# A weighted sum over experts: 128 consecutive tokens per partition, one weights transfer, longer store runs and a reshaped tail

## The chip, the cores and the metric

The kernel runs on one core of a Trainium2 chip. The metric is the time of one execution on the device in microseconds (us), as the median of several runs. Beside it there is a profile of one execution, whose span is a little shorter than the measured time because it starts with the first recorded instruction. The core has a vector engine (VectorE, DVE in the profile), a scalar engine (ScalarE, ACT), GpSimd (POOL), SyncE (SP, here used to issue transfers only), and 16 DMA engines that move data between the memory outside the core (HBM) and the on-chip memory (SBUF), which has 128 partitions.

## The reference

Every token has eight expert outputs of 512 numbers and eight weights. The result is the weighted sum over the experts, all in float32.

```python
batch, seq, n_experts, expert_dim = 16, 1024, 8, 512
expert_outputs   # (16, 1024, 8, 512) float32, 268.4 MB
combine_weights  # (16, 1024, 8)      float32, 0.5 MB

def reference(expert_outputs, combine_weights):
    weights = combine_weights[..., np.newaxis]
    return np.sum(expert_outputs * weights, axis=2).astype(np.float32)   # 33.6 MB
```

There are 16 x 1024 = 16384 tokens. A token's input is 8 x 512 x 4 bytes = 16 KiB, its output 2 KiB. Each input number is used once, with one multiplication and one addition.

## The kernel before

A step handles 256 tokens: 128 partitions with two consecutive tokens (J = 2) each. Partition p of step n holds tokens 256 n + 2 p and 256 n + 2 p + 1, so one load of 4 MiB reads one contiguous piece of HBM, as 128 runs of 32 KiB, each 32 KiB behind the one before. A store writes 512 KiB as 128 runs of 4 KiB. The layout is in the three views:

```python
P = 128
J = 2
n_steps = T // (P * J)          # 64
eo_blk = expert_outputs.rearrange("b s e d -> (b s) e d").rearrange("(n p j) e d -> n p j e d", p=P, j=J)
w_blk  = combine_weights.rearrange("b s e -> (b s) e").rearrange("(n p j) e -> n p j e", p=P, j=J)
o_blk  = out.rearrange("b s d -> (b s) d").rearrange("(n p j) d -> n p j d", p=P, j=J)
in_pool  = ...   # bufs=4, 32 KiB per partition each
out_pool = ...   # bufs=4, 4 KiB per partition each
load_engines = [nc.sync, nc.scalar]
```

Loads alternate between the queues of SyncE and ScalarE and run three steps ahead. The weights of a step come in a small transfer of their own from GpSimd. The last two steps are loaded token by token:

```python
def issue_load(m):
    in_t = in_pool.tile([P, J, E, D], fp32, name="in_t")
    w_t = w_pool.tile([P, J, E], fp32, name="w_t")
    if m < n_steps - K_TAIL:                                   # K_TAIL = 2
        load_engines[m % 2].dma_start(out=in_t, in_=eo_blk[m])                 # line 56
    else:
        for j in range(J):
            load_engines[m % 2].dma_start(out=in_t[:, j], in_=eo_blk[m, :, j]) # line 59
    nc.gpsimd.dma_start(out=w_t, in_=w_blk[m])                                 # line 60
```

In 62 of the 64 steps VectorE does all the work: for each token one product and seven fused multiply-adds over 512 numbers. The store goes out on the queue that the step's load did not use.

```python
for n in range(n_steps):
    if n + LA < n_steps:                 # LA = 3
        issue_load(n + LA)
    ...                                  # the last two steps are left to the tail below
    acc = out_pool.tile([P, J, D], fp32)
    for j in range(J):
        nc.vector.tensor_scalar_mul(out=acc[:, j, :], in0=in_tile[:, j, 0, :], scalar1=w_tile[:, j, 0:1])  # line 77
        for e in range(1, E):
            nc.vector.scalar_tensor_tensor(                                                                # line 83
                out=acc[:, j, :], in0=in_tile[:, j, e, :], scalar=w_tile[:, j, e:e+1], in1=acc[:, j, :],
                op0=mult, op1=add)
    load_engines[(n + 1) % 2].dma_start(out=o_blk[n], in_=acc)                                             # line 92
```

In the last two steps ScalarE makes the products of four of the eight experts in bf16 (line 111), VectorE does the other four (lines 116 and 122), adds the bf16 products up (lines 130, 135 and 138), and each token is stored by itself on SyncE's queue (line 141).

Of the kernel before, what the change touches and what calls it, by code (L numbers as in the profile page):

```python
# [1 line left out]

# [4 lines left out]


@with_exitstack  # L10
def kernel(
    ctx: ExitStack,
    tc: tile.TileContext,
    expert_outputs: bass.AP,
    combine_weights: bass.AP,
    out: bass.AP,
):
    nc = tc.nc
    fp32 = mybir.dt.float32
    bf16 = mybir.dt.bfloat16  # L20

    B, S, E, D = expert_outputs.shape
    T = B * S
    P = 128
    J = 2
    n_steps = T // (P * J)

    eo_blk = expert_outputs.rearrange("b s e d -> (b s) e d").rearrange(
        "(n p j) e d -> n p j e d", p=P, j=J
    )  # L30
    w_blk = combine_weights.rearrange("b s e -> (b s) e").rearrange(
        "(n p j) e -> n p j e", p=P, j=J
    )
    o_blk = out.rearrange("b s d -> (b s) d").rearrange(
        "(n p j) d -> n p j d", p=P, j=J
    )

    in_pool = ctx.enter_context(tc.tile_pool(name="in_pool", bufs=4))
    w_pool = ctx.enter_context(tc.tile_pool(name="w_pool", bufs=4))
    out_pool = ctx.enter_context(tc.tile_pool(name="out_pool", bufs=4))  # L40
    prod_pool = ctx.enter_context(tc.tile_pool(name="prod_pool", bufs=2))

    ES = E // 2
    K_TAIL = 2

    load_engines = [nc.sync, nc.scalar]

    LA = 3
    in_tiles: list[bass.AP | None] = [None] * n_steps
    w_tiles: list[bass.AP | None] = [None] * n_steps  # L50

    def issue_load(m: int) -> None:
        in_t = in_pool.tile([P, J, E, D], fp32, name="in_t")
        w_t = w_pool.tile([P, J, E], fp32, name="w_t")
        if m < n_steps - K_TAIL:
            load_engines[m % 2].dma_start(out=in_t, in_=eo_blk[m])
        else:
            for j in range(J):
                load_engines[m % 2].dma_start(out=in_t[:, j], in_=eo_blk[m, :, j])
        nc.gpsimd.dma_start(out=w_t, in_=w_blk[m])  # L60
        in_tiles[m] = in_t
        w_tiles[m] = w_t

    for m in range(min(LA, n_steps)):
        issue_load(m)

    for n in range(n_steps):
        if n + LA < n_steps:
            issue_load(n + LA)
        if n >= n_steps - K_TAIL:  # L70
            continue
        in_tile = in_tiles[n]
        w_tile = w_tiles[n]
        acc = out_pool.tile([P, J, D], fp32)

        for j in range(J):
            nc.vector.tensor_scalar_mul(  # L77
                out=acc[:, j, :],
                in0=in_tile[:, j, 0, :],
                scalar1=w_tile[:, j, 0:1],  # L80
            )
            for e in range(1, E):
                nc.vector.scalar_tensor_tensor(  # L83
                    out=acc[:, j, :],
                    in0=in_tile[:, j, e, :],
                    scalar=w_tile[:, j, e : e + 1],
                    in1=acc[:, j, :],
                    op0=mybir.AluOpType.mult,
                    op1=mybir.AluOpType.add,
                )  # L90

        load_engines[(n + 1) % 2].dma_start(out=o_blk[n], in_=acc)  # L92

    tail_steps = list(range(n_steps - K_TAIL, n_steps))
    tail_accs = {}
    tail_prods = {}
    for n in tail_steps:
        acc = out_pool.tile([P, J, D], fp32, name="acc")
        prods = prod_pool.tile([P, J, E - ES, D], bf16, name="prods")
        tail_accs[n] = acc  # L100
        tail_prods[n] = prods

    for j in range(J):
        for n in tail_steps:
            in_tile = in_tiles[n]
            w_tile = w_tiles[n]
            acc = tail_accs[n]
            prods = tail_prods[n]

            for e in range(ES, E):  # L110
                nc.scalar.mul(  # L111
                    out=prods[:, j, e - ES, :],
                    in_=in_tile[:, j, e, :],
                    mul=w_tile[:, j, e : e + 1],
                )
            nc.vector.tensor_scalar_mul(  # L116
                out=acc[:, j, :],
                in0=in_tile[:, j, 0, :],
                scalar1=w_tile[:, j, 0:1],
            )  # L120
            for e in range(1, ES):
                nc.vector.scalar_tensor_tensor(  # L122
                    out=acc[:, j, :],
                    in0=in_tile[:, j, e, :],
                    scalar=w_tile[:, j, e : e + 1],
                    in1=acc[:, j, :],
                    op0=mybir.AluOpType.mult,
                    op1=mybir.AluOpType.add,
                )
            nc.vector.tensor_add(  # L130
                out=prods[:, j, 0:2, :],
                in0=prods[:, j, 0:2, :],
                in1=prods[:, j, 2:4, :],
            )
            nc.vector.tensor_add(  # L135
                out=prods[:, j, 0, :], in0=prods[:, j, 0, :], in1=prods[:, j, 1, :]
            )
            nc.vector.tensor_add(  # L138
                out=acc[:, j, :], in0=acc[:, j, :], in1=prods[:, j, 0, :]
            )  # L140
            nc.sync.dma_start(out=o_blk[n, :, j], in_=acc[:, j, :])


# [1 line left out]
_INS = ['expert_outputs', 'combine_weights']  # L145
_OUTS = [((16, 1024, 512), 'float32')]


# [23 lines left out]
```

## Time and profile before

The median of three runs is 721.33 us (721.21 to 722.09). The profile has this to say:

| What | Number |
|---|---|
| Span of the profiled execution | 720.4 us |
| VectorE busy | 644.4 us (89%), 1020 instructions |
| ScalarE busy | 11.4 us (2%) |
| GpSimd busy (issuing weights) | 35.8 us (5%) |
| HBM read / written | 268.96 MB / 33.55 MB |
| Mean DMA rate over the span | 420 GB/s |
| Loads of 4096 KB | 62, about 33 us from issue to landing |
| Stores of 512 KB | 62, about 33 us from issue to landing |
| Stores of 256 KB (tail) | 4, 3.0 us |

The profile is read in this way. "Busy" is the time in which an engine worked on an instruction. The slices cut the span into 40 equal parts and give the busy share of each in tenths; the line of GB/s is what the DMA engines moved. The chain of waits follows the work that ended last back to the start and says which engine or transfer each part of the span waited for. A group is all instructions of one line with the same operation: after the bar stand busy time in us, mean ns of one, and the idle time of the engine just before them with what ended it. A transfer's "issue to landing" includes the time in which it stood behind others in its queue.

### The profile page before, as it was taken

The page shows a single profiled execution, that of the slowest core. Times are in us where ns is not written, and L with a number is a line of the kernel's source. Part 1 is how long each engine was busy: PE and PEld are TensorE (multiplying, and loading weights), DVE is VectorE, ACT ScalarE, POOL GpSimd, SP SyncE. Part 2 cuts the span into 40 slices and gives each one's busy share as a digit, 9 for nine tenths or more (in the row PEclk, how much of TensorE's full clock was granted, in tenths as well). Part 3 has the DMA queues.
Part 4 walks back from the last instruction along what each step waited for, and adds up shares of the span by engine and source line. Part 5 has one row for each costly group of instructions (what it writes and reads, how often), then busy time and mean ns, then how long its engine had stood idle before and what let it go on. Part 6 is the DMA issues. An engine that isn't in the chain of part 4 may idle for free.

```text
span 720.4 us, 1532 instructions
## 1 busy us (share of the span) xinstructions
DVE 644.4 (89%) x1020; ACT 11.4 (2%) x17; POOL 35.8 (5%) x68
## 2 busy tenths in 40 slices
DVE  0799999999998999989998999989998999999977
ACT  0000000000000000000000000000000000000023
POOL 1000000000000000000000000000000000000000
DMA  9999999999999999999999999999999999999993
GB/s 380 437 416 451 427 426 430 427 424 439 443 431 426 426 423 431 438 436 434 431 423 426 435 430 442 432 424 427 430 429 432 442 431 428 430 425 428 433 359 120
DMA packets 21068, 302.63 MB, mean 420 GB/s; under 512 B 3136, under 2 KB 4160, under 8 KB 12608
## 3 DMA queue, kind: packets, MB, share of 16 engines
q1 hardware_dynamic: 9792, 151.52, 49.2%
q10 hardware_dynamic: 9216, 150.47, 48.9%
q0 software_dynamic: 2048, 0.53, 0.3%
q14 instruction: 12, 0.10, 0.0%
HBM read 268.96 MB, written 33.55 MB: 420 GB/s over the span
## 4 chain that ended last, share of the span: by engine, by line
DMA 63%; DVE 35%; issue 1%; DVEq 0%; SPq 0%
DMA out_dram<-acc 56%; DVE acc L83 30%; DMA in_t<-in_expert_outputs_dram 8%; DVE acc L77 3%; DVE acc L122 1%; DVE acc L138 0%; DVE prods L130 0%; DVE acc L116 0%; DVE prods L135 0%; DVEq L77 0%; DVEq L116 0%; SPq L92 0%
## 5 line engine op out<-in xcount | busy, mean ns | idle before, releaser
L83 DVE SCALAR_TENSOR_TENSOR acc<-in_t,w_t,acc 128x512 f32<-128x512 f32 x868 | 580.1, 743 | 0.0
L77 DVE TENSOR_SCALAR acc<-in_t,w_t 128x512 f32<-128x512 f32 x124 | 54.6, 482 | 66.3 <-DMA in_t<-in_expert_outputs_dram 43.4
L60 POOL DMA_DIRECT2D w_t<-in_combine_weights_dram x64 | 35.6, 556 | 637.7 <-DVE acc L83 636.9
L111 ACT ACT_TABLE_LOAD x1 | 1.3, 1283 | 690.6 <-DMA in_t<-in_expert_outputs_dram 690.6
L111 ACT ACTIVATE prods<-in_t,w_t 128x512 bf16<-128x512 f32 x16 | 10.1, 709 | 9.0 <-DMA in_t<-in_expert_outputs_dram 9.0
L122 DVE SCALAR_TENSOR_TENSOR acc<-in_t,w_t,acc 128x512 f32<-128x512 f32 x12 | 8.9, 745 | 0.0
L116 DVE TENSOR_SCALAR acc<-in_t,w_t 128x512 f32<-128x512 f32 x4 | 1.9, 481 | 5.3 <-DMA out_dram<-acc 5.3
L138 DVE TENSOR_TENSOR acc<-acc,prods 128x512 f32<-128x512 f32 x4 | 2.8, 688 | 0.0
L130 DVE TENSOR_TENSOR prods<-prods 128x1024 bf16<-128x1024 bf16 x4 | 2.7, 683 | 0.0
L135 DVE TENSOR_TENSOR prods<-prods 128x512 bf16<-128x512 bf16 x4 | 1.7, 417 | 0.0
L156 POOL MEMSET const-float32-0.0<- 128x1 f32 x1 | 0.1, 99 | 0.2 <-issue 0.2
L156 POOL MEMSET const-bfloat16-1.0<- 128x1 bf16 x1 | 0.1, 102 | 0.0
L156 POOL MEMSET const-float32-1.0<- 128x1 f32 x1 | 0.1, 99 | 0.0
L156 POOL MEMSET const-uint8-127<- 128x1 uint8 x1 | 0.1, 99 | 0.0
## 6 DMA issues: line engine op xcount, KB each, us to landing
in_t<-in_expert_outputs_dram ACTq DMA_DIRECT2D x31, 4096.0 KB, 33.5
in_t<-in_expert_outputs_dram SPq DMA_DIRECT2D x31, 4096.0 KB, 33.3
out_dram<-acc ACTq DMA_DIRECT2D x31, 512.0 KB, 33.5
out_dram<-acc SPq DMA_DIRECT2D x31, 512.0 KB, 33.4
in_t<-in_expert_outputs_dram SPq DMA_DIRECT2D x2, 2048.0 KB, 31.2
in_t<-in_expert_outputs_dram ACTq DMA_DIRECT2D x2, 2048.0 KB, 13.9
w_t<-in_combine_weights_dram POOLq DMA_DIRECT2D x64, 8.0 KB, 6.9
out_dram<-acc SPq DMA_DIRECT2D x4, 256.0 KB, 3.0
```

Source lines behind the costliest of these rows:

```text
L60: nc.gpsimd.dma_start(out=w_t, in_=w_blk[m])
L77: nc.vector.tensor_scalar_mul(out=acc[:, j, :], in0=in_tile[:, j, 0, :], scalar1=w_tile[:, j, 0:1],)
L83: nc.vector.scalar_tensor_tensor(out=acc[:, j, :], in0=in_tile[:, j, e, :], scalar=w_tile[:, j, e : e + 1], in1=acc[:, j, :], op0=mybir.Al ...
L111: nc.scalar.mul(out=prods[:, j, e - ES, :], in_=in_tile[:, j, e, :], mul=w_tile[:, j, e : e + 1],)
L116: nc.vector.tensor_scalar_mul(out=acc[:, j, :], in0=in_tile[:, j, 0, :], scalar1=w_tile[:, j, 0:1],)
L122: nc.vector.scalar_tensor_tensor(out=acc[:, j, :], in0=in_tile[:, j, e, :], scalar=w_tile[:, j, e : e + 1], in1=acc[:, j, :], op0=mybir.Al ...
L130: nc.vector.tensor_add(out=prods[:, j, 0:2, :], in0=prods[:, j, 0:2, :], in1=prods[:, j, 2:4, :],)
L135: nc.vector.tensor_add(out=prods[:, j, 0, :], in0=prods[:, j, 0, :], in1=prods[:, j, 1, :])
L138: nc.vector.tensor_add(out=acc[:, j, :], in0=acc[:, j, :], in1=prods[:, j, 0, :])
L156: nc = _bacc.Bacc("TRN2", target_bir_lowering=False, num_devices=1)
```

## The change

The layout changes: a partition owns 128 consecutive tokens (K = 128), and there are 128 partitions, so that all 16384 tokens make one block (N = 1). A load still brings two tokens for every partition, as 128 runs of 32 KiB, but these runs are now 128 x 16 KiB = 2 MiB apart in HBM. In this layout eight tokens of a partition (G = 8) are neighbours in the output, so a store can write them as one run of 16 KiB, and all weights of a partition are one run of 4 KiB, so they come in one transfer. The first product of each token moves from VectorE to ScalarE. All loads go out on SyncE's queue, most stores on ScalarE's. The last loads shrink, in the end to one expert of one token, and so do the last stores, so that little is left to do after the last bytes have come. The bf16 products of the tail are gone.

```diff
-    J = 2
-    n_steps = T // (P * J)
+    K = 128
+    G = 8
+    J = 2
+    N = T // (P * K)
...
-        "(n p j) e d -> n p j e d", p=P, j=J
+        "(n p k) e d -> n p k e d", p=P, k=K
...
-    in_pool = ctx.enter_context(tc.tile_pool(name="in_pool", bufs=4))
-    w_pool = ctx.enter_context(tc.tile_pool(name="w_pool", bufs=4))
-    out_pool = ctx.enter_context(tc.tile_pool(name="out_pool", bufs=4))
-    prod_pool = ctx.enter_context(tc.tile_pool(name="prod_pool", bufs=2))
+    in_pool = ctx.enter_context(tc.tile_pool(name="in_pool", bufs=5))
+    w_pool = ctx.enter_context(tc.tile_pool(name="w_pool", bufs=1))
+    out_pool = ctx.enter_context(tc.tile_pool(name="out_pool", bufs=2))
...
+    w_t = w_pool.tile([P, N, K, E], fp32, name="w_t")
+    chunks = [(n, k) for n in range(N) for k in range(0, K, J)]
+    last = len(chunks) - 1
+    pin = tc.keep_in_program_order
+
+    def load(i):
+        n, k = chunks[i]
+        t = in_pool.tile([P, J, E, D], fp32, name="in_t")
+        src = x[n, :, k : k + J]
+        if i < last - 6:
+            nc.sync.dma_start(out=t, in_=src)
+            return
+        for j in range(J):
+            if i == last and j == J - 1:
+                cuts = (0, 2, 4, 5, 6, 7, 8)
+            elif i >= last - 2:
+                cuts = (0, 4, 8)
+            else:
+                cuts = (0, 8)
+            for a, b in zip(cuts, cuts[1:]):
+                nc.sync.dma_start(out=t[:, j, a:b], in_=src[:, j, a:b])
...
+    def first(i):                      # acc is a tile [P, G, D]; a is the place of the chunk in it
+        for j in range(J):
+            pin(nc.scalar.mul(out=acc[:, a + j], in_=in_tiles[i][:, j, 0], mul=w_t[:, n, k + j, 0:1]))
+
+    def rest(i):
+        for j in range(J):
+            for e in range(1, E):
+                nc.vector.scalar_tensor_tensor(
+                    out=acc[:, a + j], in0=in_tiles[i][:, j, e],
+                    scalar=w_t[:, n, k + j, e : e + 1], in1=acc[:, a + j], op0=mult, op1=add)
+
+    def store(i):                      # put(queue, lo, hi) stores tokens lo to hi of acc
+        if i < last - 3:
+            if a == G - J:
+                put(nc.scalar, 0, G)
+        elif a == 2:
+            put(nc.scalar, 0, 4)
+        elif a == 4:
+            put(nc.sync, 4, 6)
+        elif a == 6:
+            put(nc.sync, 6, 7)
+            put(nc.sync, 7, 8)
...
+    AHEAD = 4
+    load(0)
+    nc.scalar.dma_start(out=w_t.rearrange("p n k e -> p n (k e)"), in_=w)
+    for i in range(1, AHEAD):
+        load(i)
+    first(0)
+    for i in range(len(chunks)):
+        if i + AHEAD <= last:
+            load(i + AHEAD)
+        if i < last:
+            first(i + 1)
+        rest(i)
+        store(i)
```

Some lines of the diff are joined or left out here; the sizes, queues and order are as they stand in it.

More of the change, by code (lines that the diff above doesn't have):

```diff
@@ L19 @@
     fp32 = mybir.dt.float32
-    bf16 = mybir.dt.bfloat16
+    mult, add = mybir.AluOpType.mult, mybir.AluOpType.add
     B, S, E, D = expert_outputs.shape
@@ L24 @@
     P = 128
+    K = 128
+    G = 8
     J = 2
-    n_steps = T // (P * J)
-    eo_blk = expert_outputs.rearrange("b s e d -> (b s) e d").rearrange(
-        "(n p j) e d -> n p j e d", p=P, j=J
-    )
-    w_blk = combine_weights.rearrange("b s e -> (b s) e").rearrange(
-        "(n p j) e -> n p j e", p=P, j=J
-    )
-    o_blk = out.rearrange("b s d -> (b s) d").rearrange(
-        "(n p j) d -> n p j d", p=P, j=J
-    )
-    in_pool = ctx.enter_context(tc.tile_pool(name="in_pool", bufs=4))
@@ L39 @@
-    w_pool = ctx.enter_context(tc.tile_pool(name="w_pool", bufs=4))
-    out_pool = ctx.enter_context(tc.tile_pool(name="out_pool", bufs=4))
-    prod_pool = ctx.enter_context(tc.tile_pool(name="prod_pool", bufs=2))
[L43 to L74, printed above, removed]
-        for j in range(J):
[L77 to L80, printed above, removed]
-            )
+    N = T // (P * K)
@@ new lines @@
+    x = expert_outputs.rearrange("b s e d -> (b s) e d").rearrange(
+        "(n p k) e d -> n p k e d", p=P, k=K
+    )
+    w = combine_weights.rearrange("b s e -> (b s) e").rearrange(
+        "(n p k) e -> p n (k e)", p=P, k=K
+    )
+    o = out.rearrange("b s d -> (b s) d").rearrange("(n p k) d -> n p k d", p=P, k=K)
+    in_pool = ctx.enter_context(tc.tile_pool(name="in_pool", bufs=5))
+    w_pool = ctx.enter_context(tc.tile_pool(name="w_pool", bufs=1))
+    out_pool = ctx.enter_context(tc.tile_pool(name="out_pool", bufs=2))
@@ new lines @@
+    w_t = w_pool.tile([P, N, K, E], fp32, name="w_t")
+    chunks = [(n, k) for n in range(N) for k in range(0, K, J)]
+    last = len(chunks) - 1
+    in_tiles = {}
+    accs = {}
+    pin = tc.keep_in_program_order
+    def load(i):
+        n, k = chunks[i]
+        t = in_pool.tile([P, J, E, D], fp32, name="in_t")
+        in_tiles[i] = t
+        src = x[n, :, k : k + J]
+        if i < last - 6:
+            nc.sync.dma_start(out=t, in_=src)
+            return
+        for j in range(J):
+            if i == last and j == J - 1:
[6 more added lines that the diff above has]
+                nc.sync.dma_start(out=t[:, j, a:b], in_=src[:, j, a:b])
@@ new lines, in acc_of @@
+    def acc_of(i):
+        n, k = chunks[i]
+        g = (n, k // G)
+        if g not in accs:
+            accs[g] = out_pool.tile([P, G, D], fp32, name="acc")
+        return accs[g], k % G
+    def first(i):
+        n, k = chunks[i]
+        acc, a = acc_of(i)
+        for j in range(J):
+            pin(
+                nc.scalar.mul(
+                    out=acc[:, a + j],
+                    in_=in_tiles[i][:, j, 0],
+                    mul=w_t[:, n, k + j, 0:1],
+                )
+            )
@@ L82 @@
+    def rest(i):
+        n, k = chunks[i]
+        acc, a = acc_of(i)
+        for j in range(J):
             for e in range(1, E):
                 nc.vector.scalar_tensor_tensor(
[L84 to L89, printed above, removed]
-                )
-        load_engines[(n + 1) % 2].dma_start(out=o_blk[n], in_=acc)
@@ L94 @@
[L94 to L141, printed above, removed]
@@ new lines, in rest, with put @@
+                    out=acc[:, a + j],
+                    in0=in_tiles[i][:, j, e],
+                    scalar=w_t[:, n, k + j, e : e + 1],
+                    in1=acc[:, a + j],
+                    op0=mult,
+                    op1=add,
+                )
+    def store(i):
+        n, k = chunks[i]
+        acc, a = acc_of(i)
+        k0 = k - a
+        def put(queue, lo, hi):
+            pin(queue.dma_start(out=o[n, :, k0 + lo : k0 + hi], in_=acc[:, lo:hi]))
+        if i < last - 3:
[8 more added lines that the diff above has]
+            put(nc.sync, 7, 8)
```

## The prediction

> **What bounds the kernel now.** I read the page's slices first, then the queue totals, then the chain of waits, then the costliest groups, and last the windows of head and tail. The slices (busy tenths of each engine in 40 equal parts of the span):
>
> ```profile
> DVE  0799999999998999989998999989998999999977
> DMA  9999999999999999999999999999999999999993
> GB/s 380 437 416 451 427 426 430 427 424 439 443 431 426 426 423 431 438 436 434 431 423 426 435 430 442 432 424 427 430 429 432 442 431 428 430 425 428 433 359 120
> ```
>
> The reader is to see two engines close to full, VectorE (DVE) and the DMA engines, and a rate that stands near 430 GB/s from the second slice to the third last. Which of the two binds is told by the chain of waits:
>
> ```profile
> DMA 63%; DVE 35%; issue 1%; DVEq 0%; SPq 0%
> ```
>
> VectorE's part of the chain is its first 130 us, when the tiles of the first loads lie ready and it runs without a pause. From 154 us on the chain goes through transfers of 33 to 34 us that are only interrupted by one 10 us step of VectorE each. Then the groups, with VectorE's two instructions and ScalarE's one in the tail:
>
> ```profile
> L83 DVE SCALAR_TENSOR_TENSOR acc<-in_t,w_t,acc 128x512 f32<-128x512 f32 x868 | 580.1, 743 | 0.0
> L77 DVE TENSOR_SCALAR acc<-in_t,w_t 128x512 f32<-128x512 f32 x124 | 54.6, 482 | 66.3 <-DMA in_t<-in_expert_outputs_dram 43.4
> L111 ACT ACTIVATE prods<-in_t,w_t 128x512 bf16<-128x512 f32 x16 | 10.1, 709 | 9.0 <-DMA in_t<-in_expert_outputs_dram 9.0
> ```
>
> VectorE waits 66.3 us in all, for transfers. One step (two tokens per partition) takes it 10.07 us, the distance of its starts in the timeline, and takes the DMA engines 4.72 MB at 430 GB/s = 11.0 us. So the DMA engines bind by about 9%, and VectorE is the next in line. The queues and the bytes:
>
> ```profile
> DMA packets 21068, 302.63 MB, mean 420 GB/s; under 512 B 3136, under 2 KB 4160, under 8 KB 12608
> q1 hardware_dynamic: 9792, 151.52, 49.2%
> q10 hardware_dynamic: 9216, 150.47, 48.9%
> q0 software_dynamic: 2048, 0.53, 0.3%
> ```
>
> 49.2 + 48.9 + 0.3 = 98.4% of 720.4 us, that is 709 us of transfer time on all 16 engines. Nothing but fewer bytes (there are none to save), a better rate or less idle time at the two ends can help. The ends, as windows (us, busy time of DVE, ACT and POOL, clock, DMA share, GB/s):
>
> ```profile
> 0.00:18.00 18.00, 0.00 (x0) 0.00 (x0) 2.46 (x8) 1.00 0.92 380
> ...
> 540.00:660.00 120.00, 109.67 (x174) 0.00 (x0) 5.90 (x11) 1.00 1.01 432
> ...
> 684.00:702.00 18.00, 12.81 (x21) 4.58 (x7) 0.00 (x0) 1.00 0.90 358
> 702.00:720.00 18.00, 13.21 (x23) 6.83 (x11) 0.00 (x0) 1.00 0.36 131
> ```
>
> At 432 GB/s the 302.63 MB take 700.5 us. The head moves 380 x 18 = 6.84 MB, worth 15.8 us, and so loses 2.2 us. The last 36 us move (358 + 131) x 18 = 8.80 MB, worth 20.4 us, and lose 15.6 us. The remaining 2 us are lost in the middle. The tail is the only place where this layout of the work has anything to give.
>
> **What the Trainium skill says.** "DMA: Bandwidth & Descriptors", section "Where 436 GB/s comes from", puts the ceiling of one core's ports at 435 GB/s; the 432 GB/s of the middle windows agrees, so a higher rate isn't to be had. The same page, "Issuing engines are not separate DMA queues", says that transfers issued from different engines run on the same 16 DMA engines; the trace agrees, since the two queues share 98% of the time and sum to that one ceiling. Putting all loads on SyncE and most stores on ScalarE therefore changes order, not capacity. "ScalarE: Activation LUTs", section "What ACT_TABLE_LOAD costs", gives 186 ns + 0.833 ns per element + 93 ns for a per-partition scale, 705 ns for 512 elements; the trace has 709. The fourth place speaks for the other side. "DMA: Bandwidth & Descriptors", section "Latency and other measured facts", row on the HBM row pitch: copies of tiles of 128 partitions x 16 KiB reached 207 GB/s per direction at a pitch of 512 KiB between the partitions' rows, 164 at 2 MiB, 103 at 4 MiB, and 214 once the pitch was no longer a power of two. Its explanation by HBM channels is called an inference there. The trace before has a pitch of 32 KiB and can neither confirm nor deny it.
>
> **The change part by part.**
>
> First, what leaves and enters the compute engines. VectorE loses 128 first products (124 + 4, 482 ns each, 400 ns apart); they become 128 ScalarE products, 128 x 709 ns = 91 us on an engine that was idle. A step of two tokens is then 14 fused instructions, 9.28 us in the chain, instead of 10.07. All of VectorE is 896 x 0.663 = 594 us. It had slack and gets more; worth nothing on the path that sets the end, except in the tail. The bf16 tail of ScalarE products and adds goes; off the path but for its last instructions.
>
> Second, weights. 64 issues on GpSimd with small packets (2048 of them, 0.3% of the time, 2.2 us) become one transfer with a run of 4 KiB per partition. At the load rate 0.52 MB are 1.2 us: 1 us saved.
>
> Third, stores. Runs of 16 KiB in place of 4 KiB; the queue has only a quarter as many store packets. Since the mixed rate of the middle is 431 to 432 GB/s already with the small runs, at most 1 us is gained. A store now stands in ScalarE's queue, not behind 4 MB loads, so it lands sooner; two output tiles, each good for four steps (44 us), are enough beside the 33 us that a store took from issue to landing before.
>
> Fourth, the tail. After the last byte of the last load come some 2 us to the landing (the last store's bytes ended near 717.3 us and it landed at 719.1), one fused instruction of 0.74 us, a store of 3.0 us to landing, and 1.3 us to the end of the span (720.4 - 719.1): 7.0 us. In that time 1.05 MB of stores move, worth 2.4 us, so 4.6 us are lost instead of 15.6. Gain 11 us.
>
> Without anything else, the sum is 700.5 + 2.2 (head) + 1 (middle) + 4.6 (tail) = 708.3 us of span, and with the 0.9 us by which the measured time exceeds the span 709 us: 1.7% faster.
>
> Fifth, the layout. A partition owns 128 tokens, so the rows of one load lie 128 x 8 x 512 x 4 B = 2 MiB apart and those of a store 256 KiB. Every load is thus 128 runs of 32 KiB at exactly the pitch of the skill's row. Loads are 268.4 MB, 621 us at 432 GB/s. If they slow by 214/164 = 1.305, they take 811 us, 190 us more: 899 us. An estimate from that page. The row was measured with as many stores as loads, both at that pitch, and with runs half as long. Here only loads have it, so I shade the stretch to 1.26, 161 us: 709 + 161 = 870 us.
>
> **The rivals.**
> - The pitch costs nothing, and the tail is what changes: 709 us, range 706 to 714. For it: the DMA engines, not HBM, set the 432 GB/s of before, and only one core runs, so HBM may have room; loads are queued several deep, so that engines can drift out of step. Against: the skill's row was seen under just that ceiling (2 x 214 = 428).
> - The pitch costs loads as much as the row says or more, if reads bear more of it than stores: 850 to 930 us and higher.
> - The pitch costs, but the long runs and deep queue of loads soften it: 740 to 850 us.
> - VectorE becomes the bound while a store shares the engines with the loads. Between stores a load comes each 9.7 us (4.19 MB at 432) against its 9.28 us. That is close, but still under, and up to four loads wait ahead; I give it 5%, and 715 us.
> - ScalarE holds up a first product because it waits in program order to issue a store. The product for the next step has been made before the store, and it has 9 us for the next two (1.4 us). Nothing.
>
> **Range and chances.** The outcome has two peaks. I hold a visible cost of the pitch for likelier, 60%, centred on 870 to 890; the other 40% lie at 705 to 735, and to be over 2% faster the time must be below 706.9, which needs the tail to lose 2 us less than I worked out: 8%. The range must span both: 706 to 925 us.
>
> **What would show it.** Pitch: the rate in the middle slices at 330 to 350 GB/s with the DMA share still near full, VectorE's busy tenths falling to 6 or 7, its idle time (some 270 us) put down to in_t, at the same bytes. No pitch effect: middle slices at 430, VectorE near 85%, and only the last two slices fuller. Weights: queue q0 gone. First product: 128 ScalarE instructions near 709 ns and none of VectorE's at 482. Tail: last store issued 4 to 5 us before the end, the last VectorE instruction within 3 us of the last landing. I would be wrong if the time stands below 735 us (the layout was harmless), or above 930 (loads suffer more than the page's mixture), or if VectorE shows no idle time at all.

## The result, and the profile after

The changed kernel takes 746.31 us (median of four runs, 744.22 to 747.92) against 721.68 us (721.21 to 722.09). The ratio is 1.034, with a 95% interval of 1.032 to 1.036: 3.4% slower, where the prediction had 20% as the likeliest outcome and a tail gain of 1.7% as the other.

The slices of the changed kernel, for VectorE, the DMA engines and the rate:

```profile
DVE  0997896978789697896988788797897978989665
DMA  9999999999999999999999999999999999999994
GB/s 360 413 427 402 426 424 430 429 419 425 420 420 427 424 432 422 425 417 423 430 424 429 418 427 424 428 436 418 431 415 431 436 413 426 408 398 329 331 251 157
```

VectorE falls from 8 or 9 tenths to between 6 and 9, so it waits more than before: its idle time is 140 us, where the prediction expected some 270. The DMA engines are still full. The rate tells two stories. In the middle it stands near 424 instead of 431 GB/s, about 2% less where the prediction had 330 to 350. In the last five slices it drops to 398, 329, 331, 251 and 157, and in all but the last of these the DMA engines are busy: they are not starved, they are slow. Before, only the last two slices were low.

The queues and the groups, as on the page:

```profile
q1 hardware_dynamic: 12096, 269.49, 88.2%
q10 hardware_dynamic: 2448, 33.03, 10.4%
...
L98 DVE SCALAR_TENSOR_TENSOR acc<-in_t,w_t,acc 128x512 f32<-128x512 f32 x896 | 605.6, 745 | 137.5 <-ACT acc L86 128.6
L86 ACT ACTIVATE acc<-in_t,w_t 128x512 f32<-128x512 f32 x128 | 86.1, 715 | 633.2 <-DMA in_t<-in_expert_outputs_dram 633.2
```

88.2 + 10.4 = 98.6% of 746.1 us are 736 us of transfer time for the same bytes that took 709 us before. The whole loss is there: 27 us more transfer time, 25 us more run time. VectorE's 128.6 us behind ScalarE are not ScalarE's doing: ScalarE itself stood waiting for loads.

The windows (us, busy time of DVE, ACT, POOL, clock, DMA share, GB/s):

```profile
300.00:420.00 120.00, 102.14 (x154) 14.67 (x22) 0.00 (x0) 1.00 1.00 425
...
660.00:690.00 30.00, 28.61 (x39) 3.65 (x6) 0.00 (x0) 1.00 1.01 353
690.00:710.00 20.00, 12.90 (x19) 1.44 (x2) 0.00 (x0) 1.00 0.99 326
710.00:728.00 18.00, 11.10 (x16) 1.44 (x2) 0.00 (x0) 1.00 0.99 255
728.00:746.00 18.00, 10.69 (x15) 1.44 (x2) 0.00 (x0) 1.00 0.46 152
```

The slow stretch is the one with the cut loads (the last seven chunks, that is the last seven pairs of tokens): 353, 326 and 255 GB/s at a DMA share of 0.99 to 1.01.

The trace also records every packet with its size and duration; a packet is one run of a partition here. "Pitch" is the distance in HBM between the rows that two neighbouring partitions read. Means in ns, loads and stores together, of both kernels, and of a run that comes next (a pitch of 127 tokens in place of 128):

```
packet      before   changed   changed, pitch 127
32 KiB       1215      1243        1219
 8 KiB          -       464         313
 4 KiB        159       212         163
```

In the changed kernel runs of 32 KiB are 2% slower than with the other pitch, runs of 8 KiB 48%. The 16 KiB runs of its loads alone take 653 against 614 ns, 6% more, while those of its stores, whose rows lie 256 KiB apart, take 611 in both. The row of 4 KiB mixes loads, stores and weights in the changed kernel, and is stores alone in the kernel before. The median packet of 32 KiB takes 1213 ns in all three: at 2 MiB some are long, not all.

### The profile page after: what moved, and what is told of

It reads as the page before. It is cut to its first block, busy times and chain, and to the rows that moved or that the text cites. A ratio compares the mean times of both kernels' runs of the same rounds, so it can differ in the third digit from the quotient of the medians.

```text
span 746.1 us, 1345 instructions
## 1 busy us (share of the span) xinstructions
DVE 605.6 (81%) x896; ACT 87.4 (12%) x129; POOL 0.2 (0%) x4
## 3 DMA queue, kind: packets, MB, share of 16 engines
q1 hardware_dynamic: 12096, 269.49, 88.2%
q10 hardware_dynamic: 2448, 33.03, 10.4%
## 4 chain that ended last, share of the span: by engine, by line
DMA 87%; DVE 11%; ACT 1%; SPq 0%; issue 0%; ACTq 0%; DVEq 0%
DMA in_t<-in_expert_outputs_dram 87%; DVE acc L98 11%; ACT acc L86 1%; SPq L62 0%; ACTq L86 0%; SPq L72 0%; DVEq L98 0%
## 5 line engine op out<-in xcount | busy, mean ns | idle before, releaser
L98 DVE SCALAR_TENSOR_TENSOR acc<-in_t,w_t,acc 128x512 f32<-128x512 f32 x896 | 605.6, 745 | 137.5 <-ACT acc L86 128.6
L86 ACT ACTIVATE acc<-in_t,w_t 128x512 f32<-128x512 f32 x128 | 86.1, 715 | 633.2 <-DMA in_t<-in_expert_outputs_dram 633.2
L86 ACT ACT_TABLE_LOAD x1 | 1.3, 1283 | 15.6 <-DMA in_t<-in_expert_outputs_dram 15.6
```

The costliest lines, as they stand in the source:

```text
L86: nc.scalar.mul(out=acc[:, a + j], in_=in_tiles[i][:, j, 0], mul=w_t[:, n, k + j, 0:1],)
L98: nc.vector.scalar_tensor_tensor(out=acc[:, a + j], in0=in_tiles[i][:, j, e], scalar=w_t[:, n, k + j, e : e + 1], in1=acc[:, a + j], op0=mult,
```

## The experiments

Ratios are to the kernel before, timed beside each run, with 95% intervals.

**A pitch that is no power of two.** The rows of a load lie 127 tokens apart. This reads some tokens twice and leaves others out; nothing else changes.

```diff
-        src = x[n, :, k : k + J]
+        flat = expert_outputs.rearrange("b s e d -> (b s) e d")
+        src = flat[k : k + 127 * P].rearrange("(p q) e d -> p q e d", q=127)[:, 0:J]
```

> The changed kernel with one number altered: the partitions' rows of a load lie 127 tokens apart (2 MiB less 16 KiB) instead of 128, so it reads some tokens twice and leaves others out; sizes, runs, queues, order, stores and weights stay. Theory A (the power-of-two pitch makes the runs of the 16 DMA engines collide in HBM, little for runs of 32 KiB, much for those of 8 KiB and less): the middle back to 430 GB/s and the tail windows from 660 us on no longer at 250 to 350 GB/s, 708 to 714 us in all. Theory B (small loads and the two-queue order are slow in themselves): 743 to 748 us, nothing changes. Theory C (rows far apart are slow, power of two or not): 743 to 748 us as well.

Measured: 717.67 us, ratio 0.995 (0.993 to 0.996). Its windows:

```profile
480.00:600.00 120.00, 102.56 (x155) 14.67 (x22) 0.00 (x0) 1.00 1.00 432
600.00:660.00 60.00, 54.06 (x80) 7.61 (x11) 0.00 (x0) 1.00 1.00 427
660.00:690.00 30.00, 28.97 (x41) 4.33 (x6) 0.00 (x0) 1.00 1.01 424
690.00:710.00 20.00, 19.29 (x27) 2.16 (x3) 0.00 (x0) 1.00 0.74 293
```

Changing the pitch by 16 KiB in 2 MiB gives 28.6 us back, in the middle (432) and in the tail (424 where there were 353). Theories B and C fall: loads of the same small sizes ran at 424 GB/s here, and rows 16 KiB less than 2 MiB apart cost nothing in the middle. But 717.7 is 4 us more than A's upper edge, and the last line shows where: a DMA share of 0.74 with VectorE at 19.29 of 20 us. Something else sets the end there; the last experiment comes back to it.

**Whole loads in the tail, at both pitches.**

```diff
-        if i < last - 6:
+        if i <= last:
```

> The changed kernel with its 2 MiB pitch, but the last seven loads are whole (4 MiB, runs of 32 KiB) like all others. Theory A: the last 86 us no longer run at 250 to 350 GB/s; what is left is the 2% of the middle, and a longer end because 14 fused instructions (9.4 us) and the stores follow the last landing: 728 to 736 us. Theory B (small loads in themselves): the same. If the tail's loss were the stores or the waits of SyncE on earlier landings rather than the short runs: 745 us or more.

> Pitch of 127 tokens (some tokens read twice, others left out) and the last seven loads whole: the counterpart, without the power of two, of the run with whole loads at 2 MiB (733.7 us). The difference is what the pitch costs loads of 32 KiB runs alone. If the 2% of the middle is all: 12 to 15 us less, 719 to 722 us, and the cutting of the tail is worth 2 to 4 us against the 717.7 us with cut loads. If it is nearer 733 us, whole loads cost the tail as much as the pitch cost it.

Measured: 733.73 us at 2 MiB (ratio 1.017, 1.015 to 1.018), 721.41 us at 127 tokens (1.000, 0.999 to 1.001). Both are as expected. With the two runs above they make a square:

| us | 2 MiB | 127 tokens | the pitch costs |
|---|---|---|---|
| cut tail | 746.3 | 717.7 | 28.6 |
| whole tail | 733.7 | 721.4 | 12.3 |
| cutting brings | -12.6 | +3.7 | |

The pitch costs whole loads 12.3 us, and the cutting of the tail, meant to save, turns from a gain of 3.7 into a loss of 12.6 us. The windows of the run with whole loads at 2 MiB, in the stretch that had 353 and 326:

```profile
660.00:690.00 30.00, 26.61 (x41) 4.00 (x6) 0.00 (x0) 1.00 1.00 423
690.00:710.00 20.00, 13.88 (x22) 2.67 (x4) 0.00 (x0) 1.00 1.01 423
```

**Other pitches.** First 8 tokens per partition, rows 128 KiB apart:

```diff
-    K = 128
+    K = 8
```

> The changed kernel with 8 consecutive tokens per partition instead of 128: rows of a load 128 KiB apart, rows of a store 16 KiB apart (one contiguous piece), weights still in one transfer but in runs of 256 bytes; tail cuts, queues and order stay. Theory A: 708 to 714 us. Theory B: 740 us or more. Theory C: 708 to 714 us; together with the pitch of 127 tokens it tells A from C.

Measured: 733.09 us, ratio 1.016 (1.014 to 1.017), neither theory's number. The slices and a line of the issues (KB each, us to landing):

```profile
GB/s 379 430 366 192 394 423 432 430 434 430 431 429 435 434 434 430 438 432 422 440 429 434 430 430 431 434 435 432 432 436 422 440 427 437 423 429 429 424 419 141
...
w_t<-in_combine_weights_dram ACTq DMA_DIRECT2D x1, 512.0 KB, 53.1
```

The loads and the tail are at full rate; the loss is a hole in slices three to five. The weights landed only after 53 us, and no sum can be made before that, so no input buffer came free. With 8 tokens the weights are 2048 runs of 256 bytes, on a queue beside the loads. The repair is to issue them first, on the loads' own queue:

```diff
-    load(0)
-    nc.scalar.dma_start(out=w_t.rearrange("p n k e -> p n (k e)"), in_=w)
+    nc.sync.dma_start(out=w_t.rearrange("p n k e -> p n (k e)"), in_=w)
+    load(0)
```

> 8 tokens per partition (rows 128 KiB apart), with the weights' transfer issued first on SyncE's queue, ahead of the loads, instead of on ScalarE's queue beside them. Theory: the run with 8 tokens lost 14 us only because its weights, 2048 runs of 256 bytes, took turns with 32 KiB packets and landed at 54 us; ahead of the loads they land by 6 us. Then it equals the run with a pitch of 127 tokens: 717 to 720 us, with no dip in the first slices. Rival (a pitch of 128 KiB or runs of 16 KiB side by side in HBM cost something too): 725 us or more.

Measured: 718.56 us, ratio 0.996 (0.994 to 0.997). As expected, and the issue line has the weights landing after 4 us:

```profile
w_t<-in_combine_weights_dram SPq DMA_DIRECT2D x1, 512.0 KB, 4.2
```

So the hole came from where the weights stood (queue and order were changed together). Then 32 and 64 tokens (512 KiB and 1 MiB), with the weights where the change has them:

```diff
-    K = 128
+    K = 32      # and, in another run, K = 64
```

> The changed kernel with 32 tokens per partition: rows of a load 512 KiB apart, weights in four runs of 1 KiB per partition beside the loads, everything else as changed. Theory A with collisions only from 1 or 2 MiB on: loads of all sizes at full rate, weights land by 40 us, which costs the start a few us: 718 to 726 us. If collisions are there already at 512 KiB: the tail's 8 KiB packets are slow here too, 730 us or more.

> The changed kernel with 64 tokens per partition: loads 1 MiB apart, two blocks, weights in two runs of 2 KiB per partition, everything else as changed. With 32 tokens (512 KiB) all loads of the tail ran at full rate. If the collisions begin above 1 MiB: 717 to 721 us and a tail at 420 GB/s. If they begin at 1 MiB: between the two, 725 to 740 us, with packets of the tail's short loads slower than at 512 KiB.

Measured: 720.07 us (0.998, 0.998 to 0.999) and 721.09 us (0.999, 0.999 to 1.000). Weights landed after 42 and 26 us. The packet records have 8 KiB packets at 313 and 314 ns. So the loss of the tail begins between 1 and 2 MiB, and at 1 MiB only the first three slices, 54 us, are slower (349, 420 and 414 GB/s).

**The layout alone, on the kernel before.**

```diff
-        "(n p j) e d -> n p j e d", p=P, j=J
+        "(p n j) e d -> n p j e d", p=P, j=J     # weights and output likewise
```

> The kernel before with nothing but its layout changed to 128 consecutive tokens per partition: loads in runs of 32 KiB 2 MiB apart, stores in runs of 4 KiB 256 KiB apart, two queues, tail as before. Theory A: the middle loses about 2% (10 to 15 us) and the tail with its 16 KiB runs a few us: 732 to 745 us. Theory B: 720 to 723 us, the pitch is nothing. If the short store runs or the alternation of stores and loads in one queue disturb the loads at this pitch more: over 745 us.

Measured: 729.26 us, ratio 1.010 (1.009 to 1.012): less than theory A said. Its windows show why:

```profile
0.00:18.00 18.00, 0.00 (x0) 0.00 (x0) 2.45 (x8) 1.00 0.89 312
18.00:120.00 102.00, 90.89 (x145) 0.00 (x0) 4.87 (x8) 1.00 1.00 412
120.00:240.00 120.00, 112.58 (x179) 0.00 (x0) 6.76 (x12) 1.00 1.01 429
240.00:360.00 120.00, 110.58 (x175) 0.00 (x0) 5.87 (x11) 1.00 1.01 431
```

The loads start at 312 GB/s and stand at 429 to 431 from 120 us on, where the kernel before had 429 to 432: most of the loss lies in the first 120 us. The changed kernel at the same pitch stays at 419 to 427 in its windows from 18 to 660 us. The next seven runs ask for the difference.

**What keeps the middle slow.** One edit each:

```diff
-                put(nc.scalar, 0, G)                          # changed kernel: stores behind the loads
+                put(nc.sync, 0, G)
-            if a == G - J: put(nc.scalar, 0, G)               # changed kernel: 15 stores left out
+            pass
-            if a == G - J: put(nc.scalar, 0, G)               # changed kernel: short stores
+            put(nc.scalar, a, a + J)
-            nc.sync.dma_start(out=t, in_=src)                 # changed kernel: two load queues
+            (nc.sync, nc.scalar)[i % 2].dma_start(out=t, in_=src)
-    AHEAD = 4                                                 # changed kernel: 3 loads ahead, 4 buffers
+    AHEAD = 3
-    load_engines[m % 2]                                       # before at 2 MiB: loads on SyncE,
+    nc.sync                                                   #   stores on ScalarE
-    LA = 3                                                    # the same, 4 ahead, 5 buffers
+    LA = 4
```

> The changed kernel, 2 MiB pitch, with the 15 stores of eight tokens on SyncE's queue, behind the loads, as the kernel before had its stores, instead of on ScalarE's queue beside them. Theory A2 (at 2 MiB the loads run without loss once the 16 engines have fallen into a staggered order, and each store that is mixed into the loads engine by engine disturbs that order for 10 us): the windows from 120 to 600 us rise from 424 to 429 GB/s or more, and 8 to 12 us are gained: 734 to 739 us. Rival (the 2 MiB pitch costs 2% whenever there is a load): 744 to 748 us, middle at 424.

> The changed kernel, 2 MiB pitch, without the 15 stores of eight tokens (31.5 MB of output are not written; the stores of the last chunks stay). Moving the store to the loads' own queue did not help, so the question is what the 2% of the middle is. Theory A3 (loads alone settle into an order without collisions, and any 2 MiB store breaks it): slices from 60 to 580 us steady at 431 to 433 GB/s, span 746 less 73 us of stores less 10 us: 660 to 668 us. Rival (at this pitch even undisturbed loads lose 2%): slices at 420 to 426 and 671 to 676 us.

> The changed kernel, 2 MiB pitch, with a store of 512 KB after every chunk (runs of 4 KiB, 1 MiB less between stores) instead of one of 2 MiB after every fourth, on the same queue. Theory A3 with the length of a store as the cause (the kernel before at 2 MiB pitch had such short stores and lost nothing from 240 us on): the middle windows at 429 to 431 GB/s, 734 to 740 us. Rival (each store disturbs once, however short, so four times as many disturb more): middle below 424 GB/s, 746 us or more.

> The changed kernel, 2 MiB pitch, with its whole loads alternating between SyncE's and ScalarE's queues as in the kernel before; the cut loads of the tail stay on SyncE's. Theory A4 (with two queues a DMA engine takes its 32 KiB runs in turn from two loads, so that the engines are spread over two places of HBM's address range and collide less): windows from 240 to 600 us at 429 to 432 GB/s, 733 to 739 us. Rival (the queues are not the difference): 421 to 426 GB/s, 743 us or more.

> The kernel before at 2 MiB pitch with all loads on SyncE's queue and all stores of the first 62 steps on ScalarE's. Theory A4: the windows from 240 to 600 us fall from 430 to 415 to 425 GB/s and the time from 729 to 738 to 755 us. Rival (the queues are not the difference): 727 to 732 us, windows at 429 to 431.

> The changed kernel, 2 MiB pitch, with three loads ahead and four input buffers instead of four and five. Theory A5 (with more loads queued an engine that is not held up runs further ahead of the others, at 2 MiB it then meets them at other places of the address range again and again, and no lasting order forms): middle windows at 429 to 431 GB/s, 733 to 740 us. Rival (depth is not it): 421 to 426 GB/s, 744 us or more.

> The kernel before at 2 MiB pitch, all loads on SyncE's queue and stores on ScalarE's, now with four loads ahead and five input buffers. Theory A5: middle windows fall from 431 to 415 to 425 GB/s, 735 to 750 us. Rival: 724 to 729 us as with three.

| run | us | ratio, interval | GB/s in the windows 240:360, 360:480, 480:600 |
|---|---|---|---|
| changed, as it is | 746.31 | 1.034, 1.032 to 1.036 | 423, 427, 425 |
| before at 2 MiB, as above | 729.26 | 1.010, 1.009 to 1.012 | 431, 429, 431 |
| changed, stores behind the loads | 751.59 | 1.043, 1.039 to 1.047 | 418, 422, 423 |
| changed, 15 stores left out | 682.68 | one run | 421, 425, 419 |
| changed, short stores | 768.59 | 1.065, 1.059 to 1.071 | 415, 416, 416 |
| changed, two load queues | 752.57 | 1.042, 1.038 to 1.047 | 420, 416, 416 |
| before at 2 MiB, one load queue | 726.52 | 1.006, 1.004 to 1.008 | 431, 428, 431 |
| changed, three ahead | 741.15 | 1.027, 1.026 to 1.029 | 425, 425, 424 |
| before at 2 MiB, four ahead | 726.59 | 1.007, 1.006 to 1.009 | 429, 428, 431 |

None of the theories A2 to A5 holds: with the stores away the loads are as slow as with them (32 KiB packets 1242 ns against 1243); two queues do not help the changed kernel and one does not hurt the other; depth moves the changed kernel by 5 us, but its middle windows stay at 424 to 425. Short stores make it 22 us slower, and stores behind the loads 5 us. Slices of the run without the 15 stores:

```profile
GB/s 354 406 414 420 412 424 429 424 420 433 427 433 420 420 422 416 425 422 428 424 420 412 428 405 431 425 433 427 430 429 424 429 429 405 402 383 252 260 227 105
```

There is no steady 431 to 433, as theory A3 wanted, and the tail sinks further than with stores, to 227; its 680.9 us of span lie above both expectations. What lets the kernel before settle at this pitch and not the changed one is open. Two differences between the programs that were not tried are the first product on ScalarE, which shortens VectorE's step, and the weights in one transfer instead of 64.

**The end without the pitch's loss.** With a pitch of 127 tokens the tail still lost more than predicted. Pieces of its chain, in order of time (start, us, what):

```profile
645.89 0.76 DVE acc L99
646.66 0.02 issue
646.68 0.76 DVE acc L99
647.45 0.02 issue
647.47 0.76 DVE acc L99
```

The starts are 0.79 us apart, while the kernel before had 0.663. The likely reason: where a load brings two tokens, the instructions can alternate between their two sums; where it brings one token, each needs the result of the one just before it. (The order in the trace is not that of the source: in the kernel before, the first products of both tokens ran ahead of the 14 fused instructions.) Fourteen of them are then 11.0 us, more than the 9.7 us of a load. So I cut the last loads by experts across both tokens and let the instructions alternate, on top of 8 tokens per partition with the weights first:

```diff
-        for j in range(J):
-            if i == last and j == J - 1: cuts = (0, 2, 4, 5, 6, 7, 8)
-            elif i >= last - 2: cuts = (0, 4, 8)
-            else: cuts = (0, 8)
-            for a, b in zip(cuts, cuts[1:]):
-                nc.sync.dma_start(out=t[:, j, a:b], in_=src[:, j, a:b])
+        if i == last: cuts = (0, 2, 4, 5, 6, 7, 8)
+        elif i >= last - 2: cuts = (0, 2, 4, 6, 8)
+        else: cuts = (0, 4, 8)
+        for a, b in zip(cuts, cuts[1:]):
+            nc.sync.dma_start(out=t[:, :, a:b], in_=src[:, :, a:b])
...
-        for j in range(J):
-            for e in range(1, E):
+        for e in range(1, E):
+            for j in range(J):
```

> As the run with 8 tokens and the weights first, but the last seven loads are cut by experts over both tokens, not by token, so that VectorE can alternate between the two tokens' sums. Theory D (cut by token, each fused instruction waits for the one before it and they start 787 ns apart instead of 663; 14 of them take 11.0 us against 9.7 us per load, so VectorE sets the end): starts 663 ns apart to the last load, the last VectorE instruction within 4 us of the last landing, 5 to 6 us gained: 711 to 714 us. Rival (the end is set by the waits of SyncE for free transfer slots or by the landing of small loads): no gain over that run, 717 us or more.

Measured: 718.38 us, ratio 0.995 (0.994 to 0.997), no gain over 718.56. The pace did change: two lines of its timeline have twelve and four instructions in 8.04 and 2.74 us, (8.04 - 0.74) / 11 = 0.664 apart.

```profile
701.67 2.74 DVE L97 SCALAR_TENSOR_TENSOR acc<-in_t,w_t,acc 128x512 f32<-128x512 f32 x4 [1.00 <-DMA in_t<-in_expert_outputs_dram]
...
706.71 8.04 DVE L97 SCALAR_TENSOR_TENSOR acc<-in_t,w_t,acc 128x512 f32<-128x512 f32 x12 [0.38 <-DMA in_t<-in_expert_outputs_dram]
```

But up to 706 us VectorE again waits for landings; only the last twelve instructions run without a pause. The rate between 706 and 718 us, in 40 slices of 0.3 us, tells what holds the landings up:

```profile
GB/s 423 341 27 27 20 27 27 14 7 7 20 20 27 27 20 27 27 27 20 27 34 27 14 27 27 0 0 0 0 48 355 396 369 396 185 0 0 0 0 0
```

From 706.6 to 713.5 us the core moves about 27 GB/s, a sixteenth of 432: one DMA engine is still at its share of the last loads while fifteen have finished. The landing records agree. A landing is reported in sixteen parts, and for the last five load transfers fifteen parts are in by 700.3 to 705.6 us, the sixteenth 6.2 to 7.1 us later. Theory D had the pace right, and also the end of VectorE 2 us after the last load's landing, but the gain wrong; by this reading, which no run tested, the gain went to that engine. This run and the one with the weights first (718.56 us) beat the kernel before by 0.4 to 0.5%.

## Why the prediction was right or wrong

- **What binds: right.** The DMA engines bound the changed kernel as they bound the one before. VectorE stayed below it with 605.6 us busy (81% of the span), and ScalarE's 128 products took 715 ns each, against 709 in the estimate.
- **The layout, fifth step: right in its cause and direction, wrong in size.** This is the term that made the forecast miss. The prediction put one row of the Trainium skill ("DMA: Bandwidth & Descriptors", section "Latency and other measured facts": 164 GB/s at a row pitch of 2 MiB) on all loads alike: 621 us x 0.26 = 161 us. Measured by the run with 127 tokens, the pitch costs 28.6 us, a mean stretch of 1.046. With whole loads it is 12.3 us (1244 against 1218 ns a packet of 32 KiB in the two runs with whole loads). With the cut tail the packets tell where it lies: their extra time over the run with 127 tokens, spread over 16 engines, is 10.9 us for loads of 32 KiB, 2.5 us for 16 KiB, 13.3 us for 8 KiB and about 2.4 us for smaller packets, 29.1 us in all. I named the long runs as a rival that softens the cost and gave it 740 to 850 us; the measured time lies at the lower edge of that, and the rival should have been carried to its end: if long runs soften the cost, the short runs of the cut tail must sharpen it. But run length isn't the whole of it. The row's runs of 16 KiB went from 214 to 164 GB/s, 30% more time; loads in runs of 16 KiB took 6% more here. I had also read the row too widely: its 214 GB/s belong to a pitch of 4 MiB with 4 KiB added, and with 192 bytes added, no power of two either, it has 97.
- **The tail, fourth step: wrong.** It counted 4.6 us lost in place of 15.6. At 2 MiB the cut loads ran at 255 to 353 GB/s and the cutting cost 12.6 us. Without the pitch it brought 3.7 us against whole loads. The sum 700.5 + 2.2 + 1 + 4.6 had no term for VectorE's starts 0.79 us apart when loads bring one token, and none for a DMA engine that comes 4 to 9 us after the next slowest. The span with 127 tokens was 715.7 us instead of 708.3, and from 690 us on 11.5 us are lost: 25.7 us less 20 x 293 + 18 x 15 = 6.13 MB at 432 GB/s. How the loss divides between these two was not measured. The 0.9 us from span to time compared two executions; within one it is 1.8 us (747.92 against 746.1). So the 709 us without the pitch became 717.7, and with its 28.6 us 746.3.
- **Weights: the queue went as predicted, the rest incomplete.** One transfer removed queue q0 and its 2.2 us of transfer time; what that saved was not measured by itself. That its run length decides when the weights land was not seen: 15 us at 4 KiB, 26 at 2 KiB, 42 at 1 KiB and 53 at 256 bytes beside the loads, 4 ahead of them.
- **Stores and queues: nothing, as predicted,** for the time without the pitch: 432 GB/s with long stores on ScalarE's queue, as before with short ones on both. At 2 MiB it isn't nothing: short stores on ScalarE's queue cost the changed kernel 22 us.
- **The range held by its breadth.** Slower was the likelier side, at 60%, and so it came; but 746 us lies between the two peaks, 705 to 735 and 870 to 890, and only a range as wide as 706 to 925 took it in. The 870 us stood on that row, measured with runs of 16 KiB and as many stores as loads, and no run of this case had been there to scale it. The runs disagree with a carry-over of that row by size, and agree with its direction and with a loss at 2 MiB that all but goes at 512 KiB.

Not settled: what lies behind the pitch. The skill's own explanation by HBM channels is an inference; these runs show that 16 KiB less of pitch removes the loss, and that from 32 to 8 KiB the loss is larger the shorter the run, no more. Why the kernel before settles within some 120 us at the same pitch is open too.

## What to carry to other kernels

Look at the distance between the partitions' rows of a load before choosing a layout: at 2 MiB exactly it cost 12 us with runs of 32 KiB and 29 us once the tail was cut; at 1 MiB and below the cut tail lost nothing to it. Runs of 32 KiB hid most of this pitch, so that cutting the last loads gained 3.7 us at one pitch and cost 12.6 us at the other. Before cutting a tail finer, ask which engine its pieces make serial and whether all DMA engines arrive together. Try small transfers that must land first ahead of the bulk on the same queue: here that took the weights from 53 to 4 us.

## What the runs showed of the hardware that was not expected

**One DMA engine falls behind, in steps.** The trace records when each of the 16 parts of a transfer is reported, though not by which engine. In the kernel before the last part's distance to the last but one, called its lag here, grows through the run, and its steps lie where a packet of the instruction queue (8 KiB) is recorded. Seven of them:

```
instruction packet at, us        137   213   302   379   468   546   634
lag at the last load before     0.66  1.68  2.37  2.87  3.77  4.34  5.02  us
lag at the next load            1.52  2.47  3.17  3.86  4.73  5.13  5.70  us
```

The lag rises by 0.7 to 1.0 us at each, more than the 0.31 us that the packet itself takes, and falls by 0.4 us at most between them. Of eleven such packets after the start eight go with a step; at the other three (324, 346 and 433 us) the lag does not grow. In the run with 127 tokens it rises in the same way, by 0.9 to 1.0 us at four of the five packets between 335 and 621 us. That the packets are the cause is read from the coincidence and was not tested, and that it is one and the same engine is read from the steady growth. At 690 us the lag is 5.9 us. The store that the chain of the kernel before follows to 702.7 us had fifteen parts in by 690.7, and VectorE's last long wait, 5.3 us, ended with it:

```profile
673.51 29.16 DMA out_dram<-acc
```

So part of the 15.6 us that the kernel before loses at its end goes with this lag. Most of the last transfers of the run with 127 tokens have 4 to 7 us of it, those of the changed kernel 3 to 9, but there the other fifteen parts are spread over 3 to 10 us as well.

**A short-run transfer beside a bulk one lands late.** 0.52 MB of weights needed 53 us in runs of 256 bytes on a queue beside the loads and 4.2 us ahead of them on the loads' queue, at equal bytes and an equal number of runs.

**Fused instructions on one sum** started 0.787 us apart on VectorE (run with 127 tokens), and 0.664 us apart where they alternated between two sums (last run), each of 128 x 512 in float32.
